# Eight weight tiles, 32 bytes apart modulo 256: padding the split-weight buffers of an fp32r matmul kernel

## The chip, the cores and the metric

The kernel runs on one core of one Trainium2 chip. The metric is the device time of one execution in microseconds (us): the median of three runs, beside which one more execution was taken with the hardware profiler. All rows below come from that profiled execution.

## The reference

Two stacked transformer programs work on a sequence of 256 tokens with a model width of 1024. The first has two layers: a mixer of a gated delta rule and an mLSTM, then a windowed attention, each followed by a feed-forward part of width 4096 and a gated per-layer input. The second has two layers of five attention forms side by side (latent, decay-gated, block-sparse, differential and memory attention) and a convolutional feed-forward part. For what follows only the matrix products matter:

```python
proj = hn @ w_in                       # mixers: [256, 1024] @ [1024, columns]
...
return mixed.astype(hn.dtype) @ w_out
...
gate = _causal_dwconv(xn @ ffn_w_gate[l], ffn_conv_w[l], ffn_conv_b[l])
x = x + (jax.nn.silu(gate) * (xn @ ffn_w_up[l])) @ ffn_w_down[l]
```

Everything is float32. There are 234 MB of inputs, nearly all of them weights, and each weight is used once, for 256 rows of activations.

## The kernel before

**How a product is computed.** TensorE works on fp32r operands here, which hold a rounded float32. Each weight block is therefore split into two fp32r tiles: `hi` is the rounded block, and `lo` is what the rounding left out. Activations are split the same way (`aTh` and `aTl`, or pairs of `w` tiles). A product is the sum of three: high by high, high by low, low by high.

**How a weight block arrives.** `block` (line 773) loads up to 1 MB into one of two `raw` buffers. It then works in four quarters: ScalarE (ACT), or in some places VectorE (DVE), copies a quarter into `hi`; DVE subtracts it from `raw` and writes the quarter of `lo`. The four `hi` buffers and four `lo` buffers are reused in turn. 211 blocks pass through them.

**How TensorE reads the tiles.** There are two ways:

- `tmm` (line 791) makes a transposed result. 128 columns of `hi` or `lo` are loaded as the stationary operand, and 256 columns of `aTh` or `aTl` stream past as the moving operand. The profile shows these as `ps<-aTh,hi`, `ps<-aTl,hi` and `ps<-aTh,lo`, 128x256.
- `nmm` (line 804) makes a plain result. 128 columns of activations are stationary, and up to 512 columns of `hi` or `lo` stream. The profile shows these as `ps<-hi,w`, `ps<-lo,w`, `ps<-hi,aTh`, `ps<-lo,aTh` and `ps<-hi,aTl`, 128x512.

In the name `ps<-A,B` of a matmul, A is the moving operand and B the stationary one.

**One narrow block.** The block `wi0` of each of the last two layers is 356 columns wide. `stream` (called with `n=356`) reads slices `hi[:, j, :]` of 356 columns, which is 1424 bytes, so its slices begin 0, 144, 32 and 176 bytes after a multiple of 256, in turn. The quarters that ACT and DVE write for that block begin at the same four places.

**Where the tiles lie.** A tile is a run of bytes at the same address in all 128 partitions. In the built program every `hi` and `lo` buffer is 8192 bytes long, and all eight begin at a multiple of 256. So do the `raw`, `w` and `gb` buffers. `aTh` and `aTl` begin 192 bytes after a multiple of 256; the small tiles named `before` (64 bytes) and `behind` (192 bytes) put them there. The pools lie in the order `raw`, `hi`, `lo`, `w`, `gb`, small tiles.

**What sets the order of work.** All instructions are recorded first (`Recorder`), then put in order by a list scheduler (`arrange`), which has prices for each instruction and a count of buffers for each pool. For the small tiles that count is `NSM - SLACK`. Which physical buffer a tile gets is decided afterwards, in that order. Every instruction of the profile therefore has the one line 613, where the recorded calls are issued.

Of the kernel before, what the change touches and what calls it, by code (L numbers as in the profile page):

```python
# [11 lines left out]
F32R = mybir.dt.float32r  # L12
# [6 lines left out]
P = 128  # L19
# [4 lines left out]
NHL = 4  # L24
NW2 = 32
NGB = 3
NSM = 56
PARTS = 4
SLACK = 2
SLACKTIME = 4e4  # L30
# [630 lines left out]
def program(ctx, tc, A, out, dbg=None):  # L661
    nc = tc.nc
    rec = Recorder(nc)
# [6 lines left out]
    hlp = ctx.enter_context(tc.tile_pool(name="hlp", bufs=NHL))  # L670
    w2p = ctx.enter_context(tc.tile_pool(name="w2p", bufs=NW2))
    gbp = ctx.enter_context(tc.tile_pool(name="gbp", bufs=NGB))
    smp = ctx.enter_context(tc.tile_pool(name="smp", bufs=NSM))
    psp = ctx.enter_context(tc.tile_pool(name="psp", bufs=8, space=bass.MemoryType.PSUM))

    def nm(s):
        uid[0] += 1
        return f"{s}{uid[0]}"
# [5 lines left out]
    def small(w=32):  # L684
        t = rec.new("sm", NSM - SLACK, smp.tile([P, 32], F32, tag="sm", name=nm("s")))
        return t[:, :w]
# [8 lines left out]
    def f(ap):  # L695
        return ap.bitcast(F32)

    def fold(ap, a):
        return ap.rearrange("p (a b) -> p a b", a=a)
# [73 lines left out]
    def block(name, i, k, w):  # L773

        n = k * w
        raw = rec.new("raw", NRAW, rawp.tile([P, 2048], F32, tag="raw", name=nm("raw")))
        sp.dma_start(out=raw[:, :n], in_=A[name][i])
        hi = rec.new("hi", NHL, hlp.tile([P, 2048], F32R, tag="hi", name=nm("hi")))
        lo = rec.new("lo", NHL, hlp.tile([P, 2048], F32R, tag="lo", name=nm("lo")))
        for j in range(PARTS):  # L780
            c = slice(j * n // PARTS, (j + 1) * n // PARTS)
            rec.copy(hi[:, c], raw[:, c])
            dve.tensor_tensor(lo[:, c], raw[:, c], f(hi[:, c]), op=OP.subtract)
        return fold(hi[:, :n], k), fold(lo[:, :n], k)
# [34 lines left out]
    def stream(name, items, acts, kpb, halves_, n, seq, done, before=None):  # L819


        first, last = {}, {}
        for t in range(2):
            for i, tt in seq:
                if tt == t:
                    first.setdefault((items[i][0], t), i)
                    last[items[i][0], t] = i
        banks, live = {}, {}
        w = halves_ * n
        for i, t in seq:  # L830
            c, b, k0 = items[i]
            if i not in live:
                live[i] = block(name, b, kpb, w)
            if before is not None:
                before(items[i], t)
            if (c, t) not in banks:
                banks[c, t] = [acc() for _ in range(halves_)]
            hi, lo = live[i]
            for j in range(kpb):
                nmm(banks[c, t], acts(t, k0 + j), hi[:, j, :], lo[:, j, :],  # L840
                    first[c, t] == i and j == 0, last[c, t] == i and j == kpb - 1, n)
                if (j + 1) * 3 * halves_ % 6 == 0:
                    loom.step()
            if last[c, t] == i:
                done(c, t, banks.pop((c, t)))
# [242 lines left out]
    def mixer_ab(end):  # L1088
# [281 lines left out]


        hi, lo = block("w0g", 0, 8, P)
        gbank = wk(2)
        tmm(gbank, hi, lo, 1)
# [7 lines left out]
        for bi in W0T:  # L1382
            hi, lo = block("w0t", bi, 8, 256)
            ps = wk(2)
            tmm(ps, hi, lo)
            if bi >= 6:
                b_copy(bi - 6, ps)
                continue
            loom.spawn(conv(bi, ps), ("conv", bi))
            if bi == 3:  # L1390
                loom.join(*[("conv", i) for i in range(4)], "gates")
                for hp in range(2):
                    g2 = small(4)
                    dve.tensor_copy(g2[:, 0:2], st["eg", 1][:, 2 * hp : 2 * hp + 2])
                    dve.tensor_copy(g2[:, 2:4], st["eg", 1][:, 2 * hp : 2 * hp + 2])
                    st["eg2", hp] = g2
                loom.spawn(norms(), "norms")
# [752 lines left out]
```

## Time and profile before

| | us |
|---|---|
| median of 3 runs | 1400.41 |
| lowest and highest of the 3 | 1400.03, 1401.38 |
| profiled execution, its time | 1401.15 |
| span of the profiled execution, first to last instruction | 1399.4 |
| TensorE (PE) busy | 1362.3 |
| VectorE (DVE) busy | 979.3 |
| ScalarE (ACT) busy | 786.1 |
| GpSimd (POOL) busy | 119.5 |

The profiled execution is 0.74 us above the median, and 1.75 us of its time lie outside the span. A busy TensorE is not TensorE at its peak: matmuls overlap in the pipeline and their ends are modelled. How fast it goes is read from the distance between the starts of matmuls that follow each other, called their spacing here.

### The profile page before, as it was taken

To read this page: it belongs to the slowest core of one execution; us is meant where nothing else is said; L and a number is where in the kernel's file an instruction comes from. 1 tells how busy PE (TensorE), PEld (TensorE's weight loads), DVE (VectorE), ACT (ScalarE), POOL (GpSimd) and SP (SyncE) were. 2 spreads that over 40 slices of the span, in tenths; PEclk is the share of its full clock that TensorE was granted. 3 is DMA by queue.
4 is the path that set the end of the run, shared out by engine and by line. 5 is a ranking of instruction groups with operands and counts; after the bars stand their busy time and mean duration, and the time that the engine had idled before them with its cause. 6 is when DMAs were issued, how large, how long until landed. Compare 5 with 4: busy or idle time off the path is not lost.

```text
span 1399.4 us, 22914 instructions
## 1 busy us (share of the span) xinstructions
PE 1362.3 (97%) x8767; PEld 1200.1 (86%) x8774; DVE 979.3 (70%) x2182; ACT 786.1 (56%) x1800; POOL 119.5 (9%) x132
## 2 busy tenths in 40 slices
PE   6999999999999999999998999999999899999998
PEld 6899889999777799998787788999998777899997
DVE  6994875665677866666787797575667778566664
ACT  5674564444545754444575795454446678365443
POOL 0000220000010010000025210000001610000000
PEclk9999999999999999999999999999999999999999
DMA  8332354455543454445554333455544432345553
GB/s 318 137 131 99 130 210 181 181 193 201 193 164 123 139 208 181 181 181 211 200 207 168 134 107 138 162 200 179 209 171 162 173 128 92 120 152 211 181 187 115
DMA packets 36398, 236.35 MB, mean 169 GB/s; under 512 B 4160, under 2 KB 4416, under 8 KB 10176
## 3 DMA queue, kind: packets, MB, share of 16 engines
q1 hardware_dynamic: 36288, 234.88, 46.2%
q8 instruction: 69, 1.13, 0.3%
q14 instruction: 41, 0.34, 0.1%
HBM read 233.82 MB, written 1.05 MB: 168 GB/s over the span
## 4 chain that ended last, share of the span: by engine, by line
PE 83%; DVE 7%; ACT 4%; POOL 2%; DMA 2%; issue 1%; SPq 0%; ACTq 0%; DVEq 0%
PE ps L613 83%; DVE w L613 4%; ACT w L613 2%; POOL s L613 2%; DMA raw<-in_w0t 2%; DVE lo L613 1%; DVE s L613 1%; ACT hi L613 1%; DVE h L613 1%; DMA raw<-in_wi 0%; ACT L613 0%; ACT aTh L613 0%; DVE aTl L613 0%; SPq L613 0%; DVE hi L613 0%
## 5 line engine op out<-in xcount | busy, mean ns | idle before, releaser
L613 ACT ACTIVATE hi<-raw 128x512 fp32r<-128x512 f32 (+1 forms) x793 | 436.5, 619 | 296.7 <-PE ps L613 241.0
L613 DVE TENSOR_TENSOR lo<-raw,hi 128x512 fp32r<-128x512 f32 (+2 forms) x844 | 524.5, 677 | 55.9 <-ACT hi L613 52.4
L613 PE MATMUL ps<-hi,w 128*128 128x512 f32 (+1 forms) x1272 | 378.9, 395 | 0.0
L613 PE MATMUL ps<-aTh,hi 128*128 128x256 f32 x1256 | 317.5, 281 | 0.1
L613 PE MATMUL ps<-aTl,hi 128*128 128x256 f32 x1256 | 317.2, 280 | 0.0
L613 PE MATMUL ps<-aTh,lo 128*128 128x256 f32 x1256 | 313.5, 280 | 0.2 <-DVE lo L613 0.2
L613 PEld LDWEIGHTS ps<-hi,w 128*128 128x128 f32 x1272 | 225.1, 188 | 34.4 <-issue 1.2
L613 PEld LDWEIGHTS ps<-aTh,hi 128*128 128x128 f32 x1256 | 224.7, 188 | 10.5 <-ACT hi L613 0.7
L613 PEld LDWEIGHTS ps<-aTh,lo 128*128 128x128 f32 x1256 | 223.6, 189 | 10.1 <-DVE lo L613 0.9
L613 PEld LDWEIGHTS ps<-aTl,hi 128*128 128x128 f32 x1256 | 225.1, 188 | 8.3 <-issue 0.4
L613 PE MATMUL ps<-lo,w 128*128 128x512 f32 (+1 forms) x636 | 207.5, 394 | 0.0
L613 ACT ACTIVATE w<-ps 128x512 f32<-128x512 f32 (+3 forms) x261 | 126.1, 525 | 124.5 <-PE ps L613 116.3
L613 PE MATMUL ps<-lo,aTh 128*128 128x512 f32 (+2 forms) x480 | 147.4, 369 | 6.1 <-DVE lo L613 6.1
L613 PE MATMUL ps<-hi,aTh 128*128 128x512 f32 (+2 forms) x480 | 147.5, 370 | 2.1 <-ACT aTh L613 1.2
L613 PE MATMUL ps<-hi,aTl 128*128 128x512 f32 (+2 forms) x480 | 147.0, 370 | 0.1
L613 DVE CAST hi<-raw 128x512 fp32r<-128x512 f32 x51 | 21.8, 426 | 174.2 <-PE ps L613 174.2
L613 POOL TENSOR_TENSOR s<-s,nhalf 128x1 f32<-128x1 f32 (+6 forms) x60 | 83.9, 1407 | 585.4 <-DVE s L613 583.5
L613 ACT ACTIVATE w<-w 128x512 fp32r<-128x512 f32 (+5 forms) x143 | 74.8, 533 | 98.0 <-DVE w L613 95.6
L613 PEld LDWEIGHTS ps<-lo,w 128*128 128x128 f32 x636 | 113.6, 188 | 17.3 <-issue 0.7
L613 PE MATMUL ps<-cf,w 128*128 128x128 f32 (+1 forms) x572 | 96.0, 281 | 18.3 <-DMA cf<-in_cf 11.2
L613 PE MATMUL ps<-w,w 128*128 128x128 f32 (+9 forms) x912 | 108.3, 299 | 0.4 <-ACT w L613 0.2
L613 PEld LDWEIGHTS ps<-w,w 128*128 128x128 f32 (+4 forms) x912 | 88.9, 172 | 18.4 <-issue 7.0
(105 smaller groups left out, 1175.7 us busy)
## 6 DMA issues: line engine op xcount, KB each, us to landing
raw<-in_wu SPq DMA_DIRECT2D x32, 1024.0 KB, 4.8
raw<-in_wd SPq DMA_DIRECT2D x32, 1024.0 KB, 5.0
raw<-in_fg SPq DMA_DIRECT2D x22, 1024.0 KB, 4.8
raw<-in_fu SPq DMA_DIRECT2D x22, 1024.0 KB, 4.8
raw<-in_fd SPq DMA_DIRECT2D x22, 1024.0 KB, 4.8
raw<-in_wi SPq DMA_DIRECT2D x20, 1024.0 KB, 4.8
raw<-in_w0t SPq DMA_DIRECT2D x10, 1024.0 KB, 5.9
raw<-in_wo SPq DMA_DIRECT2D x10, 1024.0 KB, 4.8
```

Source lines behind the costliest of these rows:

```text
L613: getattr(self.engines[op.eng], call)(*args, **kwargs)
```

## The change

The `hi` and `lo` tiles get eight columns more, which nothing reads or writes. A buffer is then 8224 bytes long instead of 8192, so the eight buffers begin 0, 32, 64, 96 (`hi`) and 128, 160, 192, 224 bytes (`lo`) after a multiple of 256. What lies behind them (`w`, `gb`) moves by 256 bytes in all. To make room, the small tiles lose one of their 56 buffers.

```diff
-NSM = 56
+NSM = 55
...
         raw = rec.new("raw", NRAW, rawp.tile([P, 2048], F32, tag="raw", name=nm("raw")))
         sp.dma_start(out=raw[:, :n], in_=A[name][i])
-        hi = rec.new("hi", NHL, hlp.tile([P, 2048], F32R, tag="hi", name=nm("hi")))
-        lo = rec.new("lo", NHL, hlp.tile([P, 2048], F32R, tag="lo", name=nm("lo")))
+        hi = rec.new("hi", NHL, hlp.tile([P, 2056], F32R, tag="hi", name=nm("hi")))
+        lo = rec.new("lo", NHL, hlp.tile([P, 2056], F32R, tag="lo", name=nm("lo")))
```

On all five engines the built program has the same instructions in the same order as before. Every `hi`, `lo`, `w`, `raw` and `gb` tile also gets the buffer of the same number. What differs besides addresses are the small tiles' buffers, and with them the semaphore waits of 28 ACT and 6 POOL instructions, which now wait for another earlier reader. One such place on ACT, in an attention part (`w` and `s` are working and small tiles, `ps` a PSUM bank, the numbers are those of the tiles):

```order
 L613 ACTIVATE w_819,s_818<-ps_820,s_823 128x128 [waits DVE_49,PE_49,Activation_49]
 L613 ACTIVATE w_819,s_818<-ps_820,s_823 128x128
...
 L613 ACTIVATE w_910,s_901<-ps_903,s_909 128x256
 L613 ACTIVATE s_907<-s_907 128x2 [waits DVE_49]
-L613 ACTIVATE s_911<-s_911 128x2 [waits DVE_49]
+L613 ACTIVATE s_911<-s_911 128x2 [waits DVE_49,Pool_49]
```

The last instruction also waits for POOL there, for an operation that used the buffer before; nothing changed its place.

## Rows read from the trace of the kernel before

**Rows 1.** The page: busy time of each engine, and the chain that ended last.

```profile
PE 1362.3 (97%) x8767; PEld 1200.1 (86%) x8774; DVE 979.3 (70%) x2182; ACT 786.1 (56%) x1800; POOL 119.5 (9%) x132
...
PE 83%; DVE 7%; ACT 4%; POOL 2%; DMA 2%; issue 1%; SPq 0%; ACTq 0%; DVEq 0%
```

**Rows 2.** Waits: who for whom, us in total, times, longest us.

```profile
ACT hi L613 <- PE ps L613: 241.0, 64, 11.5
...
DVE w L613 <- POOL s L613: 9.8, 11, 2.2
```

**Rows 3.** Groups by form, TensorE: count, busy us, mean ns of one.

```profile
L613 PE MATMUL ps<-hi,w 128*128 128x512 f32 x1256 | 375.6, 396 | 0.0
L613 PE MATMUL ps<-aTh,hi 128*128 128x256 f32 x1256 | 317.5, 281 | 0.1
...
L613 PE MATMUL ps<-lo,w 128*128 128x512 f32 x628 | 205.0, 394 | 0.0
...
L613 PE MATMUL ps<-hi,aTh 128*128 128x512 f32 x320 | 109.5, 409 | 1.9 <-ACT aTh L613 1.0 <-ACT hi L613 0.9
```

**Rows 4.** Groups by form, TensorE, between 1300 and 1380 us.

```profile
L613 PE MATMUL ps<-aTl,hi 128*128 128x256 f32 x146 | 39.7, 278 | 0.0
...
L613 PE MATMUL ps<-hi,w 128*128 128x512 f32 x86 | 25.2, 395 | 0.0
L613 PE MATMUL ps<-lo,w 128*128 128x512 f32 x43 | 12.4, 395 | 0.0
```

**Rows 5.** Timeline of TensorE from 278.38 us: start, length, form.

```profile
278.38 0.28 PE L613 MATMUL ps<-aTh,lo 128*128 128x256 f32 x1
...
281.56 0.40 PE L613 MATMUL ps<-lo,w 128*128 128x512 f32 x1
```

**Rows 6.** Timeline of TensorE from 1369.74 us.

```profile
1369.74 0.28 PE L613 MATMUL ps<-aTl,hi 128*128 128x256 f32 x1
...
1370.98 0.63 PE L613 MATMUL ps<-hi,w 128*128 128x512 f32 x2
```

**Rows 7.** Timeline of TensorE from 386.87 us.

```profile
386.87 0.40 PE L613 MATMUL ps<-hi,aTl 128*128 128x512 f32 x1
...
389.91 0.40 PE L613 MATMUL ps<-lo,aTh 128*128 128x512 f32 x1
```

**Rows 8.** Timeline of TensorE from 1383.52 us.

```profile
1383.52 1.98 PE L613 MATMUL ps<-hi,w 128*128 128x512 f32 x8
...
1390.77 1.07 PE L613 MATMUL ps<-lo,w 128*128 128x512 f32 x4
```

**Rows 9.** Windows: stretch, length, busy us (count) by engine, granted clock, DMA share, GB/s.

```profile
278.40:281.50 3.10, 3.10 (x28) 3.10 (x27) 3.10 (x6) 1.58 (x4) 0.00 (x0) 1.00 0.48 177
386.90:389.90 3.00, 3.00 (x14) 2.44 (x13) 3.00 (x6) 0.02 (x1) 0.00 (x0) 1.00 0.00 0
1369.80:1370.90 1.10, 1.10 (x12) 1.10 (x12) 1.10 (x3) 0.65 (x2) 0.00 (x0) 1.00 0.44 112
```

**Rows 10.** Timeline of TensorE, the 356-column block.

```profile
714.18 0.49 PE L613 MATMUL ps<-hi,aTh 128*128 128x356 f32 x2
...
720.55 0.39 PE L613 MATMUL ps<-lo,w 128*128 128x512 f32 x1
```

**Rows 11.** Groups by form, ACT and DVE, the split of weights.

```profile
L613 DVE TENSOR_TENSOR lo<-raw,hi 128x512 fp32r<-128x512 f32 x816 | 512.0, 684 | 52.0 <-ACT hi L613 48.5
L613 ACT ACTIVATE hi<-raw 128x512 fp32r<-128x512 f32 x765 | 425.2, 625 | 288.6 <-PE ps L613 241.0 <-DMA raw<-in_w0t 10.5 <-DMA raw<-in_wg 7.2
...
L613 DVE TENSOR_TENSOR lo<-raw,hi 128x356 fp32r<-128x356 f32 x16 | 7.8, 521 | 3.9 <-ACT hi L613 3.9
...
L613 ACT ACTIVATE hi<-raw 128x356 fp32r<-128x356 f32 x16 | 6.8, 489 | 8.1 <-DMA raw<-in_wi 7.5 <-DVE h L613 0.6
...
L613 DVE TENSOR_TENSOR lo<-raw,hi 128x256 fp32r<-128x256 f32 x4 | 1.5, 413 | 0.0
```

## The prediction

> **What bounds the kernel now.** I read the page first. TensorE is busy for 97% of the span, and the chain that ended last is 83% TensorE [rows 1]. The waits say the same from the other side: the longest of ACT's waits in the table is for TensorE to release an `hi` buffer, 241.0 us in 64 times [rows 2]. The two engines that make the split tiles are ahead of TensorE, so the kernel's time is close to a sum of matmul spacings. The change leaves the order of work alone; it can move that sum only if it changes how fast TensorE reads `hi` and `lo`, or if it slows ACT and DVE so far that they lose their lead.
>
> So I looked for how long one matmul takes, start to start, and whether this depends on where its operands lie. The timeline answers the first question with two levels. From 278.38 to 281.56 us stand 27 matmuls of 256 columns, 117.8 ns apart [rows 5]; from 1369.74 to 1370.98 us stand 11 of the same three forms, 112.7 ns apart [rows 6]. The same split shows at 512 columns: 13 from 386.87 to 389.91 us are 233.8 ns apart [rows 7], and 32 from 1383.52 to 1390.77 us are 226.6 ns apart [rows 8]. Operands begin at the same places modulo 256 in both stretches of 256 columns (moving 192, stationary 0), and yet they differ by 5.1 ns. The windows show that neighbours do not decide it either [rows 9]: DVE is busy throughout in the slow stretch at 278 us and in the fast one at 1369 us, and the slow stretch at 387 us has no DMA and almost no ACT work. The granted clock is 1.00 in all three.
>
> **Where the kernel stands between the two levels.** Between 1300 and 1380 us TensorE never idles. It starts 129 matmuls of 512 columns and three forms of 256 columns, 146, 145 and 145, together 436 [rows 4]. Counting a 512 as two, 80 us / (436 + 258) gives 115.3 ns for 256 columns and 230.5 ns for 512. This is the middle of both pairs of levels.
>
> **The change part by part.**
>
> *Moving operand.* Matmuls that stream 512 columns of `hi` or `lo`: 1256 + 628 + 3 x 320 (the two further forms with `aTh` or `aTl` have the same count) = 2844 [rows 3]. Seven of the eight buffers no longer begin at a multiple of 256. The trace has such reads already, in the 356-column block, whose slices begin at 0, 144, 32 and 176: from 714.18 to 720.55 us stand 39 of them (18 rows of two and three rows of one), 163.3 ns apart [rows 10]. What would a block at multiples of 256 take? Between the spacings of 256 and 512 columns, 356 columns lie at 115.3 + 100/256 x 115.2 = 160.3 ns, and on the slow level at 117.8 + 100/256 x 116.0 = 163.1 ns. So three misplaced slices of four cost between nothing (if this stretch is one of the slow ones) and 3.0 ns a matmul. I take nothing, since 163.3 is within 0.2 ns of the slow level, which well-placed operands show too.
>
> *Stationary operand.* 3 x 1256 = 3768 matmuls of 256 columns load 128 columns of `hi` or `lo` as weights [rows 3]. No row has such a load from another place, so I bound it by the two levels. If all of them went to 112.7 the gain would be 2.6 x 3768 = 9.8 us; if all went to 117.8 the loss would be 2.5 x 3768 = 9.4 us. The same for the 2844: 3.9 ns each, 11.1 us, and 3.3 ns each, 9.4 us. Together these are the outer bounds, -20.9 and +18.8 us. Between ends so evenly placed I take zero: relative places already differ between the forms (moving 0 with stationary 0 in `ps<-hi,w`, moving 0 with stationary 192 in `ps<-hi,aTh`), and both levels appear with each sort.
>
> *ACT and DVE.* 816 subtractions and 765 copies of 512 columns now work at the new places. The quarters of the 356-column block lie at 0, 144, 32 and 176 today [rows 11]. For DVE, 256, 356 and 512 columns take 413, 521 and 684 ns: 1.08 ns a column on the first step and 1.04 on the second, so the misplaced form lies within 4 ns of the straight line between the others (413 + 100 x 1.06 = 519). For ACT 489 and 625 ns are 0.87 ns a column apart, so a copy at odd places is no slower for its size. Price zero. If a copy did become 4 ns longer, 765 x 4 ns = 3.1 us would come out of the 241.0 us that ACT spends waiting for buffers [rows 2], not out of TensorE's time.
>
> *One small buffer less, and other semaphores.* No instruction moves. The 28 ACT waits name POOL operations in place of others, and POOL is busy 9% of the time [rows 1]. The waits that POOL ends today come to 9.8 us in 11 times on DVE, the longest 2.2 us [rows 2]; the buffers are taken in turn over 55 instead of 56, so a reuse comes one small tile sooner. I take zero; one wait that became as long as the longest would add 2.2 us.
>
> *`w` and `gb`.* They move by a whole 256 bytes, so their places modulo 256 stay. Zero.
>
> The sum is 0 on the profiled 1401.15 us (a span of 1399.4 and 1.75 outside it). The median of the runs is 0.74 lower, so I predict 1400.4 us.
>
> **The rivals.**
>
> *Faster: the slow level is a collision of TensorE's two read streams, and spreading the tiles thins it out.* For it: two levels 5 to 7 ns apart that no other engine explains, and weight loads, busy for 86% of the span [rows 1], run beside the matmuls' streams. Against it: tiles at equal places show both levels [rows 5, 6]. If half of the slow matmuls changed over, the gain is half of 20.9: about 1390. All of it: 1379.5. It decides from 0.8 ns a matmul on (2.8 us / 3768). [...]
>
> *Slower: a stream that begins off a multiple of 256 (or of 64) pays for a broken first stretch.* This is the 356-column block read the other way. 3.0 ns over three quarters of its slices is 4.0 ns for each misplaced read; 7/8 x 2844 x 4.0 = 10.0 us, so 1410.4. If weight loads paid the same, 7/8 x 3768 x 4.0 = 13.2 us more, 1423.6. For it: 163.3 is above the 160.3 of the middle. Against it: the slow level explains it without any price on the place, and DVE and ACT show none. It decides from 1.1 ns a read (2.8 / (7/8 x 2844)). [...]
>
> *No change, since nothing on the path reads differently.* This is the forecast.
>
> **How the numbers follow.** A measurement of this kernel tells about 0.2%, 2.8 us, from no change: the three runs span 1.35 us. I give 0.46 to no change, 0.27 to the faster rival and 0.27 to the slower one; the two levels prove that something unexplained acts on TensorE's reads, so more than half goes to a change, and nothing in the rows says which sign is likelier. The likeliest case's own range is 1397.6 to 1403.2. For eight in ten the range reaches past the middle of the faster rival and the first price of the slower one: 1389 to 1411. Beyond lie the full -20.9 us and the price on weight loads too.
>
> **What would show each step right or wrong.** Unchanged: a window of 1300 to 1380 us again has some 565 matmuls, and the groups `lo<-raw,hi` and `hi<-raw` keep 684 and 625 ns. Faster: more stretches at 112.7 and 226.6 ns, at first where a pair of operands lies at different places. Slower: spacings at 512 columns above 233.8 ns, and worse for one buffer than another. If the small tiles matter, a new wait of ACT for POOL appears in the table of waits. The prediction is wrong at its root if the level on which a stretch runs is set by the operands' places after all.

## The result, and the profile after

The changed kernel takes 1412.42 us (median of 4 runs, 1411.57 to 1414.06) against 1400.74 (4 runs), a ratio of 1.0089 with a 95% interval of 1.0076 to 1.0102. It is 11.7 us slower. The profiled execution took 1412.59 us, its span is 1410.8.

The page after, busy times and the chain, beside [rows 1]:

```profile
PE 1374.9 (97%) x8767; PEld 1207.0 (86%) x8774; DVE 979.7 (69%) x2182; ACT 786.9 (56%) x1800; POOL 118.8 (8%) x132
...
PE 87%; DVE 5%; ACT 3%; POOL 2%; issue 1%; DMA 1%; SPq 0%; ACTq 0%; DVEq 0%
```

TensorE's busy time grew by 12.6 us, with the same number of instructions; DVE and ACT by less than 1 us each. TensorE is 87% of the chain. The waits after, beside [rows 2]:

```profile
ACT hi L613 <- PE ps L613: 248.9, 64, 11.8
...
DVE w L613 <- POOL s L613: 9.9, 11, 2.2
```

ACT waits 7.9 us longer for TensorE, and no new wait for POOL has come. What the span holds besides TensorE's busy time has not grown either (37.1 us before, 35.9 after). So nobody makes TensorE wait more; TensorE itself is slower. Its groups by form, the same ones as in [rows 3]:

```profile
L613 PE MATMUL ps<-hi,w 128*128 128x512 f32 x1256 | 378.2, 398 | 0.0
L613 PE MATMUL ps<-aTh,hi 128*128 128x256 f32 x1256 | 319.8, 283 | 0.0
...
L613 PE MATMUL ps<-lo,w 128*128 128x512 f32 x628 | 206.3, 396 | 0.0
...
L613 PE MATMUL ps<-hi,aTh 128*128 128x512 f32 x320 | 109.4, 409 | 1.8 <-ACT aTh L613 1.0 <-ACT hi L613 0.7
```

Products of 512 columns with `w` (375.6 to 378.2 us, 205.0 to 206.3) and those of 256 columns with `aTh` (317.5 to 319.8) have grown; the products with `aTh` as weights have not (109.5 to 109.4). But a busy time hides most of a spacing, since matmuls overlap: those of 256 columns above are busy for 283 ns each, and their class starts one every 118.1 ns (from the whole trace, below). The window of 1300 to 1380 us that the prediction named, again by form:

```profile
L613 PE MATMUL ps<-aTh,hi 128*128 128x256 f32 x150 | 41.6, 281 | 0.0
L613 PE MATMUL ps<-aTl,hi 128*128 128x256 f32 x150 | 41.2, 280 | 0.0
L613 PE MATMUL ps<-aTh,lo 128*128 128x256 f32 x151 | 40.7, 280 | 0.0
L613 PE MATMUL ps<-hi,w 128*128 128x512 f32 x78 | 22.9, 395 | 0.0
L613 PE MATMUL ps<-lo,w 128*128 128x512 f32 x38 | 11.3, 395 | 0.0
```

The bare count, 567, looks like the 565 of before, but the mixture has moved: counting a 512 as two it is 80 us / (451 + 232) = 117.1 ns a unit, against 115.3 from [rows 4].

To compare like with like I then took three stretches, each of matmuls of one class that TensorE does without a break, the same instructions in both kernels: 111 spacings of products of 512 columns with activations as weights (`A`), 77 of 512 columns with `w` as weights (`W`), and 136 of 256 columns with `hi` or `lo` as weights (`T`). Each window goes from the start of the second matmul of such a stretch to the start of its last one. (The count in the row can be one to three higher than the spacings, since it holds neighbours that overlap the window: in `W` before, a matmul is busy for 390 ns and starts 227.1 ns after the one before.) Windows of the kernel before, `A`, `W`, `T`:

```profile
core 0: us, PE busy (x) PEld busy (x) DVE busy (x) ACT busy (x) POOL busy (x), PEclk, DMA share, GB/s
416.04:441.46 25.42, 25.42 (x112) 20.88 (x111) 16.68 (x33) 11.58 (x23) 2.19 (x6) 1.00 0.52 187
1039.89:1057.38 17.49, 17.49 (x78) 14.46 (x77) 12.58 (x23) 8.71 (x20) 0.00 (x0) 1.00 0.56 187
1251.72:1267.15 15.43, 15.43 (x137) 15.43 (x137) 10.34 (x20) 8.60 (x17) 0.00 (x0) 1.00 0.73 273
```

The same three of the changed kernel:

```profile
417.45:443.24 25.79, 25.79 (x112) 20.84 (x111) 16.77 (x33) 11.71 (x23) 2.17 (x6) 1.00 0.53 186
1046.97:1064.80 17.83, 17.83 (x79) 14.45 (x77) 13.10 (x23) 9.52 (x22) 0.00 (x0) 1.00 0.56 200
1260.06:1276.25 16.19, 16.19 (x138) 16.19 (x137) 10.15 (x20) 8.47 (x17) 0.00 (x0) 1.00 0.68 260
```

With 111, 77 and 136 spacings the lengths 25.42, 17.49 and 15.43 us make 229.0, 227.1 and 113.5 ns before; 25.79, 17.83 and 16.19 us make 232.3, 231.6 and 119.0 after. The granted clock is 1.00 in all six rows. So TensorE starts every class of matmul later after the one before, at the same clock, and with nobody to wait for.

The same sum over the whole trace, pair by pair of matmuls of one class that follow each other without a break in both kernels, says where the time went: `T` rose from 115.8 to 118.1 ns a matmul, 7.4 us over 3199 pairs; `W` from 229.7 to 232.3, 3.6 us over 1415; `A` from 229.8 to 232.0, 1.7 us over 753. That is 12.7 us, against a span that is 11.4 us longer.

### The profile page after: what moved, and what is told of

Read it like the earlier page. It is cut to its first block, busy times and chain, and to the rows that moved or that the text cites. A ratio compares the mean times of both kernels' runs of the same rounds, so it can differ in the third digit from the quotient of the medians.

```text
span 1410.8 us, 22915 instructions
## 1 busy us (share of the span) xinstructions
PE 1374.9 (97%) x8767; PEld 1207.0 (86%) x8774; DVE 979.7 (69%) x2182; ACT 786.9 (56%) x1800; POOL 118.8 (8%) x132
## 4 chain that ended last, share of the span: by engine, by line
PE 87%; DVE 5%; ACT 3%; POOL 2%; issue 1%; DMA 1%; SPq 0%; ACTq 0%; DVEq 0%
PE ps L613 87%; DVE w L613 2%; POOL s L613 2%; ACT w L613 2%; DVE s L613 1%; ACT hi L613 1%; DVE lo L613 1%; DMA cf<-in_cf 1%; DVE h L613 1%; DMA raw<-in_wi 0%; ACT L613 0%; ACT aTh L613 0%; SPq L613 0%; DVE aTl L613 0%; DVE hi L613 0%
## 5 line engine op out<-in xcount | busy, mean ns | idle before, releaser
L613 PE MATMUL ps<-aTh,hi 128*128 128x256 f32 x1256 | 319.8, 283 | 0.0
```

The source lines that it names most:

```text
L613: getattr(self.engines[op.eng], call)(*args, **kwargs)
```

## The experiments

All kernels have the same instructions in the same order as the kernel before; only the places of tiles differ (and, where a line says so, where in its tile something is written). Tiles were moved with unused tiles in pools of one buffer. Places are bytes modulo 256; before they are `hi` and `lo` 0, `w` 0, `aTh` and `aTl` 192. The diffs are against the kernel before and show the lines that matter: most of those that open the pools `pad0` to `pad3` are left out, and `NSM` is 55 in all but the two that name it. The kernel before was timed again beside each set, so its median differs a little (1400.17, 1400.11, 1400.81 and 1401.11 us). Differences in us are between medians; a ratio and its 95% interval come from all executions of both kernels, and can differ from the medians' in the last digit.

**First set: which place?** Two theories: own place (a split tile costs by the place at which it begins) and spread (what costs is that tiles lie at different places, not at which).

Padding behind, the split tiles unmoved:

```diff
     hlp = ctx.enter_context(tc.tile_pool(name="hlp", bufs=NHL))
+    pad2 = ctx.enter_context(tc.tile_pool(name="pad2", bufs=1))
+    pad2.tile([P, 64], F32, name="pad2t")
```

> The hi and lo tiles as before (all eight at a multiple of 256), but 55 small buffers and w and gb 256 bytes further on, as in the change: what the change does besides the tiles' places. Own place (a read that begins off a multiple of 64 pays for itself) and spread (what costs is that the tiles lie at different places) both expect the time of before, 1400.5 us within 0.2%. A theory that the moved w tiles or the small tiles' waits cost the time expects about 1412.

Measured: 1401.70 us, ratio 1.0005 (0.9994 to 1.0017). The small buffer less, the changed semaphores and the shift of `w` and `gb` by 256 bytes cost nothing that can be measured. In the table below, the spacing of `W` is the same with `w` 256 bytes further on (227.1 ns), which is why places are counted modulo 256.

All eight split tiles at 32:

```diff
+    pad0.tile([P, 8], F32, name="pad0t")
     hlp = ctx.enter_context(tc.tile_pool(name="hlp", bufs=NHL))
+    pad2.tile([P, 56], F32, name="pad2t")
```

> All eight tiles begin 32 bytes after a multiple of 256; w and gb as in the change. Own place: every read of hi and lo is now off a multiple of 64, twice as many as in the change (four tiles of eight), so twice its 11.7 us, about 1424. Spread: the tiles are all alike, so 1400.5 within 0.2%.

Measured: 1415.91 us, ratio 1.0106 (1.0085 to 1.0126), against 1400.17 of before: 15.7 us slower with all eight tiles at equal places. Spread is not needed for the loss, and own place, which had asked for about 1424, missed the size.

Steps of 64, so that the tiles lie at 0, 64, 128 and 192:

```diff
-NSM = 56
+NSM = 53
...
-        hi = rec.new("hi", NHL, hlp.tile([P, 2048], F32R, tag="hi", name=nm("hi")))
+        hi = rec.new("hi", NHL, hlp.tile([P, 2064], F32R, tag="hi", name=nm("hi")))
```

(`lo` likewise.)

> Tiles 64 bytes apart: hi at 0, 64, 128, 192 and lo at 0, 64, 128, 192 modulo 256; 53 small buffers. Own place: all reads begin at a multiple of 64, so 1400.5 within 0.2%. Spread: four places instead of eight, as in the change about 1412, at the least 1406.

Measured: 1411.01 us, ratio 1.0072 (1.0051 to 1.0093). Multiples of 64 are no cure, so own place modulo 64 falls.

`hi` at 0 and `lo` at 128, by a pool of its own for `lo`:

```diff
     hlp = ctx.enter_context(tc.tile_pool(name="hlp", bufs=NHL))
+    pad1.tile([P, 32], F32, name="pad1t")
+    lop = ctx.enter_context(tc.tile_pool(name="lop", bufs=NHL))
+    pad2.tile([P, 32], F32, name="pad2t")
...
-        lo = rec.new("lo", NHL, hlp.tile([P, 2048], F32R, tag="lo", name=nm("lo")))
+        lo = rec.new("lo", NHL, lop.tile([P, 2048], F32R, tag="lo", name=nm("lo")))
```

> hi tiles at 0 and lo tiles at 128 modulo 256: two places, both multiples of 64. Own place: 1400.5 within 0.2%. Spread: each chain of matmuls goes back and forth between hi and lo, so there is a change of place in it as in the change itself; some of the 11.7 us, 1404 to 1412.

Measured: 1400.30 us, ratio 1.0004 (0.9993 to 1.0015). Tiles at two different places, 128 bytes apart, cost nothing in sum here. The sum hides opposite parts: `W` takes 17.75 us in its window against 17.49, while `T` gains over the whole trace (114.9 ns a matmul against 115.8). Spread, which asked for 1404 to 1412, falls with this run and the one at 32; own place modulo 64 has fallen with the run before. Two theories remain: own place modulo 128, and one that the next set names.

**Second set: own place, or the distance to the other operand?** Every product has two operands in memory, a split tile and either an activation tile or a `w` tile. The distance theory says that what counts is how far these two begin apart.

All eight split tiles at 64 (`pad0` of 16 columns, `pad2` of 48):

> All eight split tiles begin at 64 modulo 256, activations stay at 192 and w at 0. Distance theory (what counts is how far the two streams of a product lie apart modulo 128: 64 between split tiles and activations is good, nearer is bad): the distance becomes 0 modulo 128, so the products with activations slow down, 1409 to 1416 us. Own-place theory modulo 128 (a split tile at 0 or 128 is good, any other place costs): 1411 to 1416 us. Own place modulo 64: 1400.5 us.

Measured: 1414.78 us, ratio 1.0106 (1.0089 to 1.0123). Both theories said so. Its windows, `A`, `W`, `T`:

```profile
418.05:443.84 25.79, 25.79 (x112) 20.91 (x111) 16.76 (x33) 11.72 (x23) 2.15 (x6) 1.00 0.51 185
1047.89:1065.51 17.62, 17.62 (x78) 14.46 (x77) 12.74 (x23) 8.87 (x21) 0.00 (x0) 1.00 0.55 187
1260.72:1277.04 16.32, 16.32 (x139) 16.32 (x138) 10.25 (x20) 8.58 (x17) 0.00 (x0) 1.00 0.68 258
```

Split tiles, `w` and activations all moved by 32:

```diff
-    cpool.tile([P, 16], F32, name="before")
+    cpool.tile([P, 24], F32, name="before")
...
-    cpool.tile([P, 48], F32, name="behind")
+    cpool.tile([P, 40], F32, name="behind")
...
+    pad0.tile([P, 8], F32, name="pad0t")
     hlp = ctx.enter_context(tc.tile_pool(name="hlp", bufs=NHL))
     w2p = ctx.enter_context(tc.tile_pool(name="w2p", bufs=NW2))
+    pad3.tile([P, 56], F32, name="pad3t")
```

> Split tiles, w tiles and activations all begin 32 bytes later than before (32, 32, 224), so every distance between them is as before. Distance theory: 1400.5 us. Own-place theory: as with the split tiles alone at 32, 1414 to 1417 us.

Measured: 1399.51 us, ratio 0.9999 (0.9989 to 1.0009). No tile of these products begins where it did, and the time is that of before: own place falls.

Split tiles unmoved, only the activations at 0 (`before` of 32 columns, `behind` of 32, `pad2` of 64):

> Split tiles and w tiles stay at 0, the activations move from 192 to 0 modulo 256. Distance theory: the distance to the split tiles becomes 0, 1409 to 1416 us. Own place of the split tiles: 1400.5 us.

Measured: 1414.85 us, ratio 1.0096 (1.0075 to 1.0117). The loss comes back with not one split tile moved. Its three windows, `A`, `W`, `T`:

```profile
418.72:443.89 25.17, 25.17 (x113) 20.84 (x111) 16.60 (x33) 11.51 (x23) 2.21 (x6) 1.00 0.55 189
1049.57:1067.05 17.48, 17.48 (x79) 14.46 (x77) 12.40 (x22) 8.26 (x19) 0.00 (x0) 1.00 0.53 177
1262.13:1278.44 16.31, 16.31 (x138) 16.31 (x137) 10.30 (x20) 8.66 (x17) 0.00 (x0) 1.00 0.68 258
```

`T` went from 15.43 to 16.31 us (119.9 ns), `W`, which doesn't touch the activations, is as before, and `A` became a little faster (226.8 ns).

Split tiles at 64 and activations at 0 (both edits together), so that their distance is as before:

> Split tiles at 64 and activations at 0 modulo 256, w tiles at 0: the distance between split tiles and activations is 64 modulo 128 as before, that to the w tiles is 64 instead of 0. Distance theory: the products with activations are as before, so 1400 to 1406 us, depending on what the products with w make of 64. Own place modulo 128: as all split tiles at 64, 1411 to 1416 us.

Measured: 1399.99 us, ratio 1.0000 (0.9988 to 1.0012). Two moves of which each alone costs 14.7 us cancel. Of the two theories, only the one on distance says so. Windows, `A`, `W`, `T`:

```profile
413.75:439.17 25.42, 25.42 (x112) 20.84 (x111) 16.69 (x33) 11.59 (x23) 2.21 (x6) 1.00 0.53 189
1036.30:1053.93 17.63, 17.63 (x78) 14.46 (x77) 13.08 (x23) 9.46 (x22) 0.00 (x0) 1.00 0.55 201
1248.69:1264.13 15.44, 15.44 (x139) 15.44 (x137) 10.08 (x20) 8.31 (x17) 0.00 (x0) 1.00 0.73 272
```

`A` and `T`, whose distances are those of before, have their spacings of before; `W`, now at 64, takes what `A` takes at 64 (229.0 ns).

**Third set: one pair at a time.** `w` alone at 32 (`pad2` of 8 columns, `pad3` of 56 behind `w2p`):

> Split tiles stay at 0 and activations at 192; only the w tiles move, from 0 to 32 modulo 256. Distance theory for every pair of operands: the 512-column products that hold w as the stationary operand go from 229.8 to about 232.7 ns, as they did with the split tiles at 32; 1480 such spacings x 2.9 ns = 4.3 us, so 1404.5 us, and the 256-column products with activations keep 115.7 ns. Rival, only the distance between split tiles and activations counts: 1400.2 us.

Measured: 1406.99 us, ratio 1.0038 (1.0027 to 1.0049). That is 6.2 us more than 1400.81 where 4.3 were expected; the interval of the difference begins at 3.8. Windows `A`, `W`, `T`:

```profile
416.07:441.50 25.43, 25.43 (x113) 20.85 (x112) 16.71 (x33) 11.59 (x23) 2.21 (x6) 1.00 0.52 187
1042.23:1060.20 17.97, 17.97 (x79) 14.47 (x77) 12.94 (x23) 9.45 (x22) 0.00 (x0) 1.00 0.56 197
1255.10:1271.12 16.02, 16.02 (x139) 16.02 (x137) 10.12 (x20) 8.48 (x17) 0.00 (x0) 1.00 0.70 263
```

Activations alone at 224 (`before` of 24 columns, `behind` of 40, `pad2` of 64):

> Split tiles and w tiles stay at 0, the activations move from 192 to 224 modulo 256. Distance theory: the distance to the split tiles becomes 96 modulo 128, where the changed kernel's products of 256 columns took 118.3 ns against 115.7: 3200 x 2.6 ns = 8.3 us, and the 512-column products with activations lose up to 3 ns each, 767 x 3 = 2.3 us; 1408 to 1411 us, with the products with w as before. Rival, only equal places (0) are bad: 1400.2 us.

Measured: 1410.55 us, ratio 1.0074 (1.0055 to 1.0094). Windows:

```profile
416.96:442.86 25.90, 25.90 (x112) 20.80 (x111) 16.80 (x33) 11.75 (x23) 2.14 (x6) 1.00 0.52 185
1044.34:1061.82 17.48, 17.48 (x78) 14.46 (x77) 12.94 (x23) 9.21 (x22) 0.00 (x0) 1.00 0.57 198
1256.81:1272.90 16.09, 16.09 (x138) 16.09 (x137) 10.03 (x20) 8.32 (x17) 0.00 (x0) 1.00 0.69 262
```

The two are mirror images. With `w` moved, `W` rises to 17.97 us (233.4 ns) and `A` stays at 25.43; with the activations moved, `A` rises to 25.90 (233.3 ns) and `W` stays at 17.48. The whole times agree with that: 6.2 us for `w` and 9.7 for the activations make 15.9, and moving all split tiles by 32, which shifts both distances by 32 (the other way), cost 15.7. Each of the three is known to within 1.5 to 3 us, so it is in part luck that they meet so closely. (In the first of the two, `T` stands at 117.8 ns without having been touched; more on that below.) Groups by form say it over the whole span, `w` moved:

```profile
L613 PE MATMUL ps<-hi,w 128*128 128x512 f32 x1256 | 378.8, 398 | 0.0
L613 PE MATMUL ps<-aTh,hi 128*128 128x256 f32 x1256 | 317.5, 281 | 0.4 <-ACT hi L613 0.4
```

and activations moved:

```profile
L613 PE MATMUL ps<-hi,w 128*128 128x512 f32 x1256 | 375.6, 396 | 0.0
L613 PE MATMUL ps<-aTh,hi 128*128 128x256 f32 x1256 | 319.9, 283 | 0.0
```

Against 375.6 and 317.5 in [rows 3], each edit moves, of these two forms, only the one whose distance it changes.

**Fourth: can the distances be better than before?** `A` ran faster with activations at 0. The activations were therefore given two places: 192 for stages with `T` products, and 64 bytes later for stages that only hold them as weights.

```diff
-    aTh = cpool.tile([P, 8, 256], F32R, name="aTh")
-    aTl = cpool.tile([P, 8, 256], F32R, name="aTl")
+    aTh = cpool.tile([P, 2064], F32R, name="aTh")
+    cpool.tile([P, 48], F32, name="between")
+    aTl = cpool.tile([P, 2064], F32R, name="aTl")
+    at0, at64 = [tuple(fold(x[:, o : o + 2048], 8) for x in (aTh, aTl)) for o in (0, 16)]
...
-        stream("w1n", items, a_T, 4, 1, 512, lagged(6, 2), nat_done)
+        stream("w1n", items, a_T64, 4, 1, 512, lagged(6, 2), nat_done)
```

(`wg`, `wi0` and `wi` likewise, and the writes ahead of them.)

> The activations stay at 192 modulo 256 (distance 64 modulo 128) in stages whose products of 256 columns stream them; in the stages that only hold them as the stationary operand under 512 columns (and the 356-column block) they are written 64 bytes later, at 0, where the run with activations at 0 had 227.6 ns instead of 229.9. Distance theory: 912 products x 2.3 ns = 2.1 us less, 1398.1 us. Rival, the 227.6 came from something else in that run: 1400.2 us.

Measured: 1400.04 us against 1400.81, ratio 0.9993 (0.9981 to 1.0004). The window `A` did what was expected, 25.18 us or 226.8 ns against 25.42; the 2.1 us over the whole kernel are inside the interval, and so is nothing at all. Inconclusive in time.

The last kernel keeps that and adds the place of `lo` at 128 for the blocks of `T` products (`lop` is again a pool of its own for `lo`):

```diff
-NSM = 56
+NSM = 47
...
-        n = k * w
+        n, o = k * w, 32 * (name[:2] in ("w0", "wu", "fg", "fu") and name not in ("w0n", "w0o"))
...
-        lo = rec.new("lo", NHL, hlp.tile([P, 2048], F32R, tag="lo", name=nm("lo")))
+        lo = rec.new("lo", NHL, lop.tile([P, 2112], F32R, tag="lo", name=nm("lo")))
...
-            dve.tensor_tensor(lo[:, c], raw[:, c], f(hi[:, c]), op=OP.subtract)
-        return fold(hi[:, :n], k), fold(lo[:, :n], k)
+            dve.tensor_tensor(lo[:, o + c.start : o + c.stop], raw[:, c], f(hi[:, c]), op=OP.subtract)
+        return fold(hi[:, :n], k), fold(lo[:, o : o + n], k)
```

> As the run with activations at two places, and in addition lo is written 128 bytes into its tile (tiles 256 bytes longer, 47 small tiles) for the blocks that the 256-column products use, and at 0 for those that 512-column products stream; order of work as before. Distance theory with the measured spacings: 256-column products with activations 114.9 ns as in the run with lo at 128, instead of 115.7, x 3195 = 2.7 us less; 512-column products with w stay at 229.8; those with activations 227.6 instead of 229.9 x 912 = 2.1 us less; 1395.6 us. Rival, the 0.85 ns of the run with lo at 128 does not belong to that place and the small tiles cost something: 1398 to 1401 us.

Measured: 1397.70 us (12 runs) against 1401.11 (17 runs), ratio 0.9974 (0.9962 to 0.9987). It is the fastest kernel of this study, 3.4 us faster than the kernel before. Windows:

```profile
414.42:439.60 25.18, 25.18 (x112) 20.84 (x111) 16.60 (x33) 11.50 (x23) 2.19 (x6) 1.00 0.55 190
1036.86:1054.34 17.48, 17.48 (x78) 14.45 (x77) 12.91 (x23) 9.03 (x21) 0.00 (x0) 1.00 0.56 190
1248.86:1264.29 15.43, 15.43 (x137) 15.43 (x137) 10.25 (x20) 8.58 (x17) 0.00 (x0) 1.00 0.72 273
```

All three classes stand at their lowest at once: 226.8, 227.0 and 113.5 ns. The expected gain of 4.8 us (1400.4 to 1395.6) came out as 3.4, and the interval (1.8 to 5.3) holds 4.8 and also the 2.4 at the near end of the rival's range. So the gain is shown, but how it divides between the two moves is not: the activations' part alone did not come clear of noise.

**All windows together.** Spacing in ns over the same three stretches (length / 111, 77 and 136), with the distance in bytes, moving minus stationary, modulo 256. Kernels in which `hi` and `lo` of one class lie at several distances are left out, but for the last:

| kernel | A: distance, ns | W: distance, ns | T: distance, ns |
|---|---|---|---|
| before | 64, 229.0 | 0, 227.1 | 192, 113.5 |
| padding behind | 64, 229.0 | 0, 227.1 | 192, 117.7 |
| all moved by 32 | 64, 228.8 | 0, 227.1 | 192, 117.8 |
| split 64, activations 0 | 64, 229.0 | 64, 229.0 | 192, 113.5 |
| `w` at 32 | 64, 229.1 | 224, 233.4 | 192, 117.8 |
| activations at 224 | 32, 233.3 | 0, 227.0 | 224, 118.3 |
| split tiles at 32 | 96, 233.4 | 32, 233.2 | 160, 118.7 |
| split tiles at 64 | 128, 232.3 | 64, 228.8 | 128, 120.0 |
| activations at 0 | 0, 226.8 | 0, 227.0 | 0, 119.9 |
| activations at two places | 0, 226.8 | 0, 227.1 | 192, 113.5 |
| and `lo` at two places | 0, 226.8 | 0, 227.0 | 192 and 64, 113.5 |

Read down a column: in `A` and `W` one distance gives one spacing in these stretches, whichever tile was moved to make it. For 512 columns 0 is best (227), 64 next (229), 128 worse (232), and 32, 96 and 224 worst (233.3). For 256 columns 0 and 128 are the worst (120.0), 160 and 224 stand between (118.3 to 118.7), and 113.5 occurs only at 192, or with `lo` at 64 beside it, though not always. Distances 160 and 192 at 512 columns, and 32, 64 and 96 at 256, were run only in mixtures, if at all.

The whole trace bears the table out, and shows where it is not the whole story. I took the spacings of every stretch with at least 12 of one class, some 650 of `A`, 680 of `W` and 2340 of `T` in each kernel. At most distances they stay within some 2 ns in nearly every stretch of a kernel: `W` at 0 in the kernel before lies between 226.6 and 228.3 ns, `T` at 224 between 117.9 and 118.8. At two distances there is a second, higher level:

- 64 at 512 columns. `A` in the kernel before is at 229 to 230 ns but for one stretch of 89 spacings at 233.3; `W` with the split tiles at 64 and the activations at 0 is at 229 to 230 but for 212 of 683 at 233.3.
- 192 at 256 columns. `T` is at about 113.5 or at 117.8. Of the spacings in stretches of 20 or more, 810 of 2108 are at the higher level in the kernel before, and 282 to 1196 in the other kernels with that distance alone. With `lo` at 128, so that `T` has 192 and 64, not one such stretch is at the higher level in either of the two kernels that have it; the slowest is at 115.7.

## Why the prediction was wrong

**The step that failed** is the pricing of both operands at zero, and in it the sentence that relative places already differ between the forms and "both levels appear with each sort". The two levels were real, and at 256 columns they do appear at equal places; from that I concluded that places don't set the spacing at all. At 512 columns the rows did not even say that: the slow stretch [rows 7] has `aTh` and `aTl` as weights, distance 64, and the fast one [rows 8] has `w`, distance 0. They are two sorts, and in no stretch of 12 or more of the kernel before was `W` above 228.3 or `A` below 228.8 ns. The runs show that the distance between the operands decides which spacings a stretch can have (in the table, at 512 columns 226.8 to 227.1 ns at 0 and 233.2 to 233.4 at 32, 96 and 224), and that a remainder which I can't explain (113.5 or 117.7 ns at distance 192) lies within that. I had compared stretches that differ in nothing and found a difference; no row held two stretches of one class in which only the distance differed. The root error that the prediction named, that the level is set by the operands' places after all, is what happened.

*The size.* The changed kernel's eight tiles can be priced from three runs, each taken whole: two tiles at 0 and 128, as in the run with `lo` at 128, 0.1 us for all; two at 64 and 192, as with all at 64, 14.7 us for all, a quarter of it 3.7; four at 32, 96, 160 and 224, as with all at 32, 15.7 for all, half of it 7.9. The sum is 11.6 us; 11.7 were measured. This is an estimate, since it takes a tile at 96, say, to cost what one at 32 does. For steps of 64 the same sum is half of 14.7, 7.3 us, against 10.8 measured, whose interval reaches from 7.1 to 13.0. The two terms put at zero can be read from the two profiled traces: the stationary term (`T`), bounded at +9.4, came to 7.4 us, and the moving term (`W` and `A`), bounded at +9.4 too, to 5.3. Both outer bounds held, and both zeros failed.

*The 356-column block* [rows 10], on which the moving term rested, is no gauge for this. After the change its tiles lie elsewhere, and the same 39 matmuls take 6.33 us, 162.3 ns each against 163.3:

```profile
718.48 0.49 PE L613 MATMUL ps<-hi,aTh 128*128 128x356 f32 x2
...
724.81 0.40 PE L613 MATMUL ps<-lo,w 128*128 128x512 f32 x1
```

Its slices go through four places in turn, before as after, so it averages over distances. That its spacing lay at the slow level was read as "no price on the place"; it was at that level while misplaced, one of its four distances to the activations (96) being among the worst at 512 columns (233.4 ns).

*The rivals.* The slower one came within about 2 us of the result (1410.4) by luck, with the wrong mechanism: streams that begin off a multiple of 256 paid nothing for it in the run with everything moved by 32 (1399.51), and streams that begin on one paid in others (activations at 0, 1414.85; `w` at 32, 1406.99). Its sign, spacings above 233.8 ns at 512 columns, did not come: the windows show 232.3 and 231.6. The faster one was nearer, in that the places of TensorE's two operands matter to each other, and had the sign wrong: the distances of before were already at or near the best ones, and spreading the tiles took most of them away. That the two streams collide is not shown; the runs show only that the spacing changes with the distance (the table above).

*ACT and DVE.* Right in the price, though two sizes of ACT's copy could not have told a price on the place from a fixed cost. The split took what it took before [rows 11], in the changed kernel by form:

```profile
L613 DVE TENSOR_TENSOR lo<-raw,hi 128x512 fp32r<-128x512 f32 x816 | 512.1, 684 | 50.3 <-ACT hi L613 46.6
...
L613 ACT ACTIVATE hi<-raw 128x512 fp32r<-128x512 f32 x765 | 425.5, 626 | 294.1 <-PE ps L613 248.9 <-DMA raw<-in_w0t 10.1 <-DMA raw<-in_wg 7.1
```

*The small tiles and `w`.* Right: the run with padding behind has both and is as before (1.0005).

*What the test missed.* The window of 1300 to 1380 us was to show "again some 565 matmuls". It showed 567, as if nothing had changed, in a kernel that is 11.7 us slower, because a window at a fixed time meets another mixture. Windows on the same instructions would have been the test.

*What stays open.* Why `T` at distance 192 runs at 113.5 ns in some stretches and at 117.8 in others, within one kernel [rows 5, 6] and on the same instructions from kernel to kernel, and why a stretch of 512 columns at distance 64 ran at 233.8 instead of 229.0 [rows 7]; whether the distance that counts is the one to a matmul's own weights or to the next ones, since all of a stretch lie alike; and what gives these distances their order. That `lo` at 128 keeps `T` off the higher level rests on the one profiled execution of each of the two kernels that have it; no run tells why.

## What to carry to other kernels

In this kernel, where TensorE streams fp32r operands almost without a break (busy for 97% of the span), the place of the moving operand relative to the stationary one, modulo 256 bytes, is a parameter worth 1%: a padding that looks harmless cost that much (1412.42 us against 1400.74), while the best distances found gained 0.3% (1397.70 us against 1401.11). The best were 0 for 512 columns (226.8 to 227.1 ns) and 192 for 256 (with `lo` at 64; 113.5 ns). Check that a new tile ahead in memory hasn't moved one partner alone. To price a suspected effect, find stretches that differ in that one thing; a difference between stretches that are alike shows that something else acts too, and says nothing against the effect. Compare windows on the same instructions, never at the same time.

## What the hardware showed unexpectedly

- The distance between two operands changes the spacing of fp32r matmuls at a granted clock of 1.00: 226.8 to 233.4 ns at 512 columns and 113.5 to 120.0 at 256, while a shift of both operands together by 32 bytes left the time as it was (1399.51 us, ratio 0.9999). The same 32 bytes for `w` alone cost 6.2 us.
- The best distance for 512 columns, 0 (226.8 to 227.1 ns), is one of the two worst for 256 (119.9 ns).
- At one distance, 192, and a granted clock of 1.00, 256 columns have two levels, 113.5 and 117.8 ns. With `lo` at 128 no stretch of 20 spacings or more stood at the higher one, in two kernels (the slowest was at 115.7).
- Writes of DVE and ACT show nothing of the kind: 684 and 626 ns at eight places, 684 and 625 at one.
